# The per-layer embedding's gate as seven half-size products, with its norm weights applied at evacuations and two schedules re-paced

## The chip, the cores and the metric

One kernel runs on 1 core of a Trainium2 chip. The metric is the device time of the program in microseconds (us), the median of several runs. One more execution is profiled; all rows below are of that one.

## The reference

A decoder block on x of 512 tokens by 1024 channels, float32. Three stages follow each other: a mixer (input projection, causal pooling and a recurrent branch, merged, times `w_o`), a gated ConvFFN (`w_up`, conv, gelu, `w_down`), and a gated per-layer input embedding. What the change touches is the last stage and its join to the second:

```
x   = x + rms_norm(hid @ w_down, g_ffn_post)
ple_gate = sigmoid(rms_norm(x, g_ple_gate) @ w_ple_gate)      # 512 x 1024 @ 1024 x 1024
ple      = rms_norm(p @ w_ple_proj, g_ple_post)               # 512 x 256 @ 256 x 1024
x   = x + ple_gate * ple
```

with `rms_norm(x, g) = x * rsqrt(mean(x*x) + eps) * g`.

## The kernel before

**Numbers.** Every float32 operand of a product is split into a high part (`hi`, rounded to fp32r by a copy on ACT) and a low part (`lo = raw - hi`, a subtraction on DVE). `mm3` (lines 196 to 200) makes each product of three matmuls: hi*hi, hi*lo, lo*hi. So each 128x1024 piece of a weight costs one load, one cast on ACT and one subtraction on DVE.

**Seven products.** `wo`, `up` and `wd` are computed by a 2x2 scheme of halves (tokens, inner channels and output channels are each cut in two) with seven products in place of eight, in the order `SERIAL = (1, 2, 5, 6, 3, 7, 4)`. Products 5, 6, 7 and 4 use sums of weight blocks. `sum_in_dram` makes these sums in DRAM with DMAs on the POOL queue, the second of each pair accumulating: those of `wo` and `up` in one go once the first rsqrt is done, those of `wd` six DMAs at a time (`SUMS_EACH`), each batch released by a step of the up loop. The left operands' forms (for instance h21-h22) are made on DVE, then split. `product` walks through one product; its two banks are the first and the second 128 tokens of a half.

**Gate stage.** It isn't one of these: for each half h of the output columns and each token tile t of 128, eight inner blocks k times three matmuls of 512 columns, then sigmoid on ACT from PSUM with the row's rstd as scale, a multiply by the embedding, an add of x and a DMA out:

```python
for h in range(2):
    for t in range(NT):
        V.scalar_tensor_tensor(v, v, rp[t], gp[:, h, :], ALU.mult, ALU.mult)
        ...
                    mm3(ps[:, a:b], x3k, pick(w, (k % 2) * S + a, (k % 2) * S + b), k == 0, k == KD - 1)
                act(o[:, a:b], ps[:, a:b], AF.Sigmoid, scale=r3[t])
```

**Join.** `x3_norm(t)` forms x after the ConvFFN for tile t (two PSUM multiplies, two squares with sums on ACT, a power on POOL, two scaled adds), multiplies it by `g_ple_gate` on DVE, and takes its rstd. `x3_tile(t)` transposes the tile on the TensorE (eight 128x128 transposes, line 858) and splits what lands in PSUM. `down_product(4, ...)` is the last product of `wd`: its first bank (tile 2) ends 18 matmuls before its second (tile 3). The TensorE's order is that of the program (a manual schedule); tiles 2 and 3 are transposed inside the gate stage, after (h, t, k) = (0, 1, 2) and after (0, 1).

**Order of the other engines.** DVE, ACT, SP and POOL are scheduled by priority at build time (`tc.high_priority`, `urgent()`), then run in that order. Weights pass through six buffers each of `raw`, `hi` and `lo`; `weight(key, ahead)` prepares the next pieces. A load waits on SP until a `raw` buffer is free, and what stands behind it in SP's queue waits too.

Of the kernel before, what the change touches and what calls it, by code (L numbers as in the profile page):

```python
# [49 lines left out]
SUMS_FROM, SUMS_EACH = 2, 6  # L50
# [31 lines left out]
def block_kernel(  # L82
# [104 lines left out]

    def sub(o, a, b):
        V.tensor_tensor(o, a, b, ALU.subtract)  # L189
# [32 lines left out]
    def rows2(w, kp, h):  # L222
# [7 lines left out]
        name: w.rearrange("(q a s p) c -> q s p a c", a=2, s=2, p=P) for name, w in (("wo", w_o), ("wd", w_down))  # L230
# [22 lines left out]
    def sums_of(name):  # L253
# [7 lines left out]
        for f, start, more in ((5, 1, 0), (7, 0, 3), (6, 5, 3), (4, 6, 2)):  # L261
# [55 lines left out]
    for h in range(2):  # L317
        for kp in range(4):
            plan(("wpg", kp, h), rows2(w_ple_gate, kp, h))
# [62 lines left out]
    def prep(key):  # L382
# [28 lines left out]
        else:  # L411
            ACT.copy(hi, raw)  # L412
            with tc.high_priority(offset=2 * URGENT if key[0] == "wpg" and key[2] == 0 else 300 if key[0] == "in" and key[1] >= 12 else 0):
                sub(lo, raw, hi.bitcast(F32))
        ready[key] = (hi, lo)
# [75 lines left out]
    sum_in_dram(chain_of(sums_of("wo"), sums_of("up")), None)  # L491
# [246 lines left out]
    def ple_tile(t):  # L738
# [8 lines left out]
        outs = [slot(), slot()]  # L747
        V.tensor_copy(outs[0], pair[0])
        ACT.copy(outs[1], pair[1])
# [37 lines left out]
    of, od = {}, {}  # L787

    def o_form(f):

        h11, h12, h21, h22 = (halves(mq[k], b) for b in range(2) for k in range(2))
        v = {1: h11, 2: h12, 4: h22}.get(f)
        if f in (5, 7):
            od[f] = quad("C", F32)[:, 0:2, :].rearrange("p a (b c) -> p (a b) c", b=2)
# [9 lines left out]
        elif f == 7:  # L804
            v = od[7]
            V.tensor_tensor(v, h11, h21, ALU.subtract)
        of[f] = quad("A").rearrange("p (s a) (b c) -> p s (a b) c", s=2, b=2)
        split(of[f][:, 0], of[f][:, 1], v)

# [6 lines left out]
    for m in range(KD):  # L816
# [5 lines left out]
        if m == KD - 1:  # L822
            o_form(1)
# [10 lines left out]
        if m == KD - 1:  # L834
            o_form(2)
# [127 lines left out]

    forms = {1: h2(0, 0), 2: h2(0, 1), 4: h2(1, 1)}
# [190 lines left out]
    x3t, r3 = {}, {}  # L1155
    x3n = {}

    def x3_norm(t, pair):
        res = [x3[t // 2][:, 2 * (t % 2) + h, :] for h in range(2)]
        with tc.high_priority(offset=URGENT if t > 1 else 0):  # L1160
            add_norm(pair, (gq[:, 0, :], gq[:, 1, :]), res)
            for h in range(2):
                x3n[t, h] = nq[t // 2][:, 2 * (t % 2) + h, :]
                V.tensor_tensor(x3n[t, h], res[h], gq[:, 2 + h, :], ALU.mult)
        s3 = rstd_of(res)
# [39 lines left out]
    nq[0] = quad("C", F32)  # L1205
    for _ in down_product(7, zd, False, tail=2):
        pass
# [3 lines left out]
    load_x3(1)  # L1211
    x3_norm(0, (c11[0], c12[0]))
    for q in down_product(4, zd, False, head=3, tail=DOWN_TAIL):
        if q == 2:
            x3_norm(1, (c11[1], c12[1]))
            nq[1], gp = hquad(), hquad()
            nc.sync.dma_start(
                gp[:, 0:2, :].rearrange("p h c -> p (h c)"), rows[G_PLE_POST : G_PLE_POST + 1, :].broadcast_to([P, D])
            )
            ple = [quad("A", F32), quad("A", F32)]  # L1220
            for a in range(2):
# [3 lines left out]
                )  # L1225
        if q >= NQ:
            x3_norm(q - NQ + 2, (zd[q - NQ], q5[:, q - NQ]))
        if 1 < q < NQ + 1:
            x3_tile(0 if q < NQ else 1)


    for h in range(2):
        for t in range(NT):
            i = 2 * (t % 2) + h
            o = temp()
            v = ple[t // 2][:, i, :]
            V.scalar_tensor_tensor(v, v, rp[t], gp[:, h, :], ALU.mult, ALU.mult)
            parts = ((0, S // 2), (S // 2, S)) if (h, t) == (1, NT - 1) else ((0, S),)
            for a, b in parts:
                ps = bank()  # L1240
                for k in range(KD):
                    if (h, t, k) == (0, 1, 3):
                        x3_tile(2)
                    w = weight(("wpg", k // 2, h))
                    q = (k % 4) * P
                    x3k = pick(x3t[t, k // 4], q, q + P)
                    mm3(ps[:, a:b], x3k, pick(w, (k % 2) * S + a, (k % 2) * S + b), k == 0, k == KD - 1)
                act(o[:, a:b], ps[:, a:b], AF.Sigmoid, scale=r3[t])
                V.tensor_tensor(o[:, a:b], o[:, a:b], ple[t // 2][:, i, a:b], ALU.mult)
                V.tensor_tensor(o[:, a:b], o[:, a:b], x3[t // 2][:, i, a:b], ALU.add)  # L1250
                nc.sync.dma_start(out[t * P : (t + 1) * P, h * S + a : h * S + b], o[:, a:b])
            if (h, t) == (0, 1):
# [78 lines left out]
```

## Time and profile before

| what | us |
|---|---|
| median of 3 runs | 736.77 (735.72 to 737.68) |
| the profiled execution's own time | 737.34 |
| its span, first to last instruction | 735.6 |
| busy: TensorE (PE) / DVE / ACT / POOL | 728.2 / 577.8 / 443.6 / 82.7 |

PE is the matmul unit, PEld its weight loads, DVE the vector engine, ACT the scalar (activation) engine, POOL the GpSimd, SP the queue that issues most DMAs. A matmul's listed duration overlaps the next one's, so its cost in a row of matmuls is the distance between starts. Engine order is fixed, so an engine that waits holds up all that stands behind.

### The profile page before, as it was taken

To read this page: it belongs to the slowest core of one execution; us is meant where nothing else is said; L and a number is where in the kernel's file an instruction comes from. 1 tells how busy PE (TensorE), PEld (TensorE's weight loads), DVE (VectorE), ACT (ScalarE), POOL (GpSimd) and SP (SyncE) were. 2 spreads that over 40 slices of the span, in tenths; PEclk is the share of its full clock that TensorE was granted. 3 is DMA by queue.
4 is the path that set the end of the run, shared out by engine and by line. 5 is a ranking of instruction groups with operands and counts; after the bars stand their busy time and mean duration, and the time that the engine had idled before them with its cause. 6 is when DMAs were issued, how large, how long until landed. Compare 5 with 4: busy or idle time off the path is not lost.

```text
span 735.6 us, 11212 instructions
## 1 busy us (share of the span) xinstructions
PE 728.2 (99%) x4281; PEld 641.8 (87%) x4281; DVE 577.8 (79%) x749; ACT 443.6 (60%) x670; POOL 82.7 (11%) x107
## 2 busy tenths in 40 slices
PE   9999999999999999999999999999999999999997
PEld 7887778888888888889999999999999888888886
DVE  4896735999646577776989999979799997788852
ACT  6746779844543334477856666666577756565721
POOL 0312112100000000120002323131210000001100
PEclk9999999999999999999999999999999999999999
DMA  8999786664788997895457798979798675768011
GB/s 328 382 309 268 166 238 175 154 198 131 267 297 267 325 327 286 306 333 180 144 191 267 176 321 234 315 206 273 253 246 297 206 250 193 266 201 270 18 58 57
DMA packets 64933, 172.53 MB, mean 235 GB/s; under 512 B 5808, under 2 KB 6448, under 8 KB 64560
## 3 DMA queue, kind: packets, MB, share of 16 engines
q1 hardware_dynamic: 50336, 129.78, 50.9%
q0 software_dynamic: 14400, 41.95, 24.1%
q8 instruction: 33, 0.54, 0.3%
q14 instruction: 20, 0.16, 0.1%
q10 hardware_dynamic: 144, 0.10, 0.0%
HBM read 155.03 MB, written 58.72 MB: 291 GB/s over the span
## 4 chain that ended last, share of the span: by engine, by line
PE 87%; DMA 7%; DVE 3%; issue 1%; ACT 1%; SPq 0%; POOL 0%; DVEq 0%; ACTq 0%
PE ps L198 28%; PE ps L199 28%; PE ps L200 28%; DMA raw<-in_w_up_dram 5%; DMA C<-in_x_dram 1%; DVE lo L189 1%; PE ps L858 1%; DVE raw L348 1%; PE ps L606 1%; DMA m<-in_x_t_dram 1%; PE ps L503 1%; DVE t L1000 1%; ACT C L486 0%; ACT hi L193 0%; SPq L403 0%
## 5 line engine op out<-in xcount | busy, mean ns | idle before, releaser
L189 DVE TENSOR_TENSOR lo<-raw,hi 128x1024 fp32r<-128x1024 f32 (+2 forms) x193 | 224.5, 1183 | 50.1 <-ACT hi L412 29.4
L198 PE MATMUL ps<-A,hi 128*128 128x256 f32 (+1 forms) x608 | 197.8, 325 | 1.1 <-ACT ps L985 1.1
L199 PE MATMUL ps<-A,hi 128*128 128x256 f32 (+1 forms) x608 | 197.1, 324 | 0.0
L200 PE MATMUL ps<-A,lo 128*128 128x256 f32 (+1 forms) x608 | 197.0, 324 | 0.0
L412 ACT CAST hi<-raw 128x1024 fp32r<-128x1024 f32 (+1 forms) x112 | 113.2, 1015 | 108.1 <-PE ps L199 43.2
L198 PEld LDWEIGHTS ps<-A,hi 128*128 128x128 f32 x608 | 114.3, 188 | 12.8 <-ACT ps L985 1.5
L200 PEld LDWEIGHTS ps<-A,lo 128*128 128x128 f32 x608 | 114.1, 188 | 10.1
L199 PEld LDWEIGHTS ps<-A,hi 128*128 128x128 f32 x608 | 114.1, 188 | 9.7
L198 PE MATMUL ps<-C,hi 128*128 128x256 f32 (+1 forms) x392 | 116.9, 298 | 0.0
L200 PE MATMUL ps<-C,lo 128*128 128x256 f32 (+1 forms) x392 | 116.6, 297 | 0.0
L199 PE MATMUL ps<-C,hi 128*128 128x256 f32 (+1 forms) x392 | 116.5, 297 | 0.0
L193 ACT CAST hi<-raw 128x1024 fp32r<-128x1024 f32 x78 | 80.6, 1052 | 33.2 <-PE ps L199 23.3
L198 PE MATMUL ps<-hi,A 128*128 128x512 f32 x224 | 87.4, 390 | 0.0
L200 PE MATMUL ps<-hi,A 128*128 128x512 f32 x224 | 87.2, 389 | 0.0
L199 PE MATMUL ps<-lo,A 128*128 128x512 f32 x224 | 87.1, 389 | 0.0
L198 PEld LDWEIGHTS ps<-C,hi 128*128 128x128 f32 x392 | 73.8, 188 | 2.8 <-ACT rb L441 0.2
L199 PEld LDWEIGHTS ps<-C,hi 128*128 128x128 f32 x392 | 73.8, 188 | 2.6
L200 PEld LDWEIGHTS ps<-C,lo 128*128 128x128 f32 x392 | 73.7, 188 | 2.5
L434 POOL TENSOR_TENSOR s<-s,mhalf 128x1 f32<-128x1 f32 (+1 forms) x21 | 15.8, 754 | 353.9 <-DVE s L447 334.6
L200 PEld LDWEIGHTS ps<-hi,A 128*128 128x128 f32 x224 | 42.0, 188 | 8.8
L199 PEld LDWEIGHTS ps<-lo,A 128*128 128x128 f32 x224 | 42.1, 188 | 8.6
L198 PEld LDWEIGHTS ps<-hi,A 128*128 128x128 f32 x224 | 42.0, 188 | 8.5
(191 smaller groups left out, 1026.2 us busy)
## 6 DMA issues: line engine op xcount, KB each, us to landing
raw<-in_w_up_dram SPq DMA_DIRECT2D x46, 512.0 KB, 7.4
wdsum<-in_w_down_dram POOLq DMA_DIRECT2D x36, 512.0 KB, 13.0
raw<-in_w_in_dram SPq DMA_DIRECT2D x32, 512.0 KB, 6.6
raw<-wdsum SPq DMA_DIRECT2D x24, 512.0 KB, 4.4
raw<-in_w_down_dram SPq DMA_DIRECT2D x18, 512.0 KB, 4.6
wosum<-in_w_o_dram POOLq DMA_DIRECT2D x12, 512.0 KB, 9.8
wdsum<-wdsum POOLq DMA_DIRECT2D x12, 512.0 KB, 12.0
parts<-hi SPq DMA_DIRECT2D x10, 512.0 KB, 3.9
```

The costliest lines, as they stand in the source:

```text
L189: V.tensor_tensor(o, a, b, ALU.subtract)
L193: last_copy[0] = ACT.copy(hi, src)
L198: PE.matmul(o, ah, bh, start=start, stop=False, **kw)
L199: PE.matmul(o, ah, bl, start=False, stop=False, **kw)
L200: PE.matmul(o, al, bh, start=False, stop=stop, **kw)
L348: V.tensor_tensor(o, a, b, ALU.add)
L412: ACT.copy(hi, raw)
L434: last_pow[0] = nc.gpsimd.tensor_tensor(y, v, mhalf[:, :n], ALU.pow).ins.name
L503: PE.matmul(rx[m], a[:, o : o + P], b, start=k == 0 and i == 0, stop=k == KD - 1 and i == 2)
L606: PE.matmul(ps, bd[pr, a, o], b[pr], start=i == 0, stop=i == 2)
L858: PE.transpose(ps[:, q * P : (q + 1) * P], a[:, q * P : (q + 1) * P], ident)
L1000: V.scalar_tensor_tensor(a[:, d:], pg[:, : S - d], c1(C_FW + (2 - d) * NJ + j), a[:, d:], ALU.mult, ALU.add)
```

## The change

- The gate's product becomes seven products of halves in the `SERIAL` order: `pg_product` runs 2 banks x 4 inner blocks x 3 matmuls for each. Its weight sums are 16 more DMAs on the POOL queue, put behind those of `wo` and `up`.
- The left operand is kept whole as `xq`, and its forms are made by `pg_form` (whole) or `pg_part` (one tile of 128 tokens).
- `g_ple_gate` is applied as a per-partition scale when the transposed tile leaves PSUM (eight ACT instructions of 128 columns for each tile in place of two casts and two subtractions); `g_ple_post` when the embedding's product leaves PSUM in `ple_tile` (two DVE multiplies in place of a DVE copy and an ACT copy).
- The low parts of weight products 7 and 4 are made by ACT (minus hi) and an accumulating DMA on the POOL queue (`BY_DMA`).
- Norms of tiles 0 and 1 move before `down_product(7)`, transposes of tile 0 into it; tile 1's go to an earlier place in `down_product(4)`; tiles 2 and 3 are transposed after the first bank of gate products 1 and 2.
- `spread_rstd` (eight small matmuls that spread the first rstd) moves from after k = 2 to after k = 7 of the first input tile.
- `SUMS_EACH` is 5 in place of 6.

```diff
+BY_DMA = 7, 4
+SUMS_PG = (5, 1, 0), (6, 5, 3), (7, 0, 3), (4, 6, 2)
-SUMS_FROM, SUMS_EACH = 2, 6
+SUMS_FROM, SUMS_EACH = 2, 5
...
-    for h in range(2):
-        for kp in range(4):
-            plan(("wpg", kp, h), rows2(w_ple_gate, kp, h))
+    for f in SERIAL:
+        for q in range(pieces["wpg"]):
+            plan(("wpg", f, q), piece_of("wpg", f, q))
...
+            if key[0] == "wpg" and key[1] in BY_DMA:
+                with tc.high_priority(offset=300):
+                    ACT.copy(hi, raw)
+                    ACT.activation(lo, hi.bitcast(F32), AF.Identity, scale=-1.0)
+                    nc.gpsimd.dma_start(lo.bitcast(F32), raw, accum_op=ALU.add)
+                ready[key] = (hi, lo)
+                return
...
-    sum_in_dram(chain_of(sums_of("wo"), sums_of("up")), None)
+    sum_in_dram(chain_of(sums_of("wo"), sums_of("up"), sums_of("wpg")), None)
...
-            if m == 0 and k == 2:
+            if m == 0 and k == KD - 1:
                 spread_rstd()
...
-        outs = [slot(), slot()]
-        V.tensor_copy(outs[0], pair[0])
-        ACT.copy(outs[1], pair[1])
+        outs = [gp[:, 2 + h, :] if t == 2 else slot() for h in range(2)]
+        for h in range(2):
+            V.tensor_tensor(outs[h], pair[h], gp[:, h, :], ALU.mult)
...
     def x3_norm(t, pair):
...
-            for h in range(2):
-                x3n[t, h] = nq[t // 2][:, 2 * (t % 2) + h, :]
-                V.tensor_tensor(x3n[t, h], res[h], gq[:, 2 + h, :], ALU.mult)
...
     def x3_tile(t):
-        xq = hquad(F32R)
         for h in range(2):
-            ps = transposed(x3n[t, h])
-            x3t[t, h] = xq[:, 2 * h, :], xq[:, 2 * h + 1, :]
-            with urgent():
-                split(*x3t[t, h], ps)
+            ps = transposed(x3[t // 2][:, 2 * (t % 2) + h, :])
+            for q in range(4):
+                with urgent():
+                    ACT.activation(
+                        xq[q % 2][:, 2 * h + q // 2, t * P : (t + 1) * P],
+                        ps[:, q * P : (q + 1) * P],
+                        AF.Identity,
+                        scale=gcol[:, 4 * h + q : 4 * h + q + 1],
+                    )
...
+    def pg_part(f, i):
...
+        v, w = pd[f][:, :, t], pf[f][:, :, :, t]
+        with tc.high_priority(offset=URGENT if f != 3 else 330):
+            if f == 3:
+                ins = V.tensor_tensor(v, v, h12, ALU.add)
+                behind(ins, low[0])
+            else:
+                V.tensor_tensor(v, *((h21, h22) if f == 5 else (v, h11)), ALU.subtract)
+            split(w[:, 0], w[:, 1], v)
...
+    def out_tile(t, h, v, a=0, b=S):
+        o = temp()[:, : b - a]
+        x3h, pl = (m[t // 2][:, 2 * (t % 2) + h, a:b] for m in (x3, ple))
+        with urgent():
+            act(o, v[:, a:b], AF.Sigmoid, scale=r3[t])
+        V.scalar_tensor_tensor(o, o, rp[t], pl, ALU.mult, ALU.mult)
+        V.tensor_tensor(o, o, x3h, ALU.add)
+        nc.sync.dma_start(out[t * P : (t + 1) * P, h * S + a : h * S + b], o)
+
+    def pg_product(f, banks, start, cols=(0, S)):
+        w = [weight(("wpg", f, q), ahead=3 if f == 3 and q else q if f == 6 else 1 + q) for q in range(2)]
+        for i in range(2):
+            for a, b in zip(cols, cols[1:]) if i else ((0, S),):
+                for k in range(4):
+                    mm3(...)
+                yield i, a, b
+
+    for i, _, _ in pg_product(1, gz, True):
+        ACT.copy(g11[i], gz[i])
+        if i == 0:
+            x3_tile(2)
+            pg_part(5, 0)
+    for i, _, _ in pg_product(2, g11, False):
+        if i == 0:
+            x3_tile(3)
+            pg_part(5, 1)
+            hold["wpg", 6, 0] = low[0] = last_sub[0]
+            for n in range(2):
+                pg_part(6, n)
...
+    for i, _, _ in pg_product(5, gd5, True):
+        ACT.copy(q5[:, i], gd5[i])
+        out_tile(i, 0, g11[i])
+        x3_rstd(2 + i)
+    for i, _, _ in pg_product(6, gz, False):
+        ins = V.tensor_tensor(g11[i], q5[:, i], gz[i], ALU.subtract)
+        if i == 0:
+            hold["wpg", 3, 1] = ins.ins.name
+            for n in range(2):
+                pg_part(3, n)
+    for i, _, _ in pg_product(3, g11, False):
+        if i == 0:
+            pg_form(7)
+        out_tile(i, 1, g11[i])
+    for i, _, _ in pg_product(7, gz, False):
+        V.tensor_tensor(q5[:, i], q5[:, i], gz[i], ALU.subtract)
+        if i == 0:
+            pg_form(4)
+        out_tile(2 + i, 1, q5[:, i])
...
+    for i, a, b in pg_product(4, gz, False, (0, HALF, S)):
+        out_tile(2 + i, 0, gd5[i] if a else gz[i], a, b)
```

## Rows read from the trace of the kernel before

**Rows 1.** The page: busy time of each engine, and the TensorE clock granted in each fortieth of the span, in tenths of full speed.
```profile
PE 728.2 (99%) x4281; PEld 641.8 (87%) x4281; DVE 577.8 (79%) x749; ACT 443.6 (60%) x670; POOL 82.7 (11%) x107
...
PEclk9999999999999999999999999999999999999999
```

**Rows 2.** What the TensorE waited for in the whole span: us in total, times, longest.
```profile
PE ps L198 <- ACT ps L985: 1.1, 2, 0.8
PE ps L216 <- DVE mhalf L210: 1.1, 1, 1.1
```

**Rows 3.** The TensorE in order of time through the gate stage: start, duration, line, operation. The stage's first matmul, its two groups of transposes, the first and the last of the 48 matmuls of 256 columns that end it.
```profile
684.64 0.39 PE L200 MATMUL ps<-hi,A 128*128 128x512 f32 x1
684.87 0.39 PE L198 MATMUL ps<-hi,h 128*128 128x512 f32 x1
...
692.36 1.04 PE L858 MATMUL ps<-ident,h 128*128 128x128 f32 x8
...
696.74 1.32 PE L858 MATMUL ps<-ident,h 128*128 128x128 f32 x8
...
725.14 0.28 PE L198 MATMUL ps<-hi,h 128*128 128x256 f32 x1
...
730.77 0.28 PE L200 MATMUL ps<-hi,h 128*128 128x256 f32 x1
```

**Rows 4.** ACT and DVE after the last matmul, in order of time.
```profile
731.09 0.47 ACT L164 ACTIVATE t<-ps,r 128x256 f32<-128x256 f32 x1 [2.40 <-PE ps L200]
...
731.59 0.42 DVE L1249 TENSOR_TENSOR t<-t,A 128x256 f32<-128x256 f32 x1 [1.99 <-ACT t L164]
732.05 0.42 DVE L1250 TENSOR_TENSOR t<-t,C 128x256 f32<-128x256 f32 x1
```

**Rows 5.** Busy time by stretch in the gate stage: stretch, its length, then PE, PEld, DVE, ACT and POOL busy (instructions), granted clock, DMA share, GB/s.
```profile
685.00:700.00 15.00, 14.96 (x75) 12.16 (x74) 13.41 (x24) 11.03 (x23) 2.86 (x3) 1.00 0.00 0
700.00:716.00 16.00, 16.00 (x72) 13.27 (x71) 8.74 (x13) 4.18 (x5) 0.00 (x0) 1.00 0.18 67
716.00:731.00 15.00, 15.00 (x90) 13.25 (x88) 4.21 (x7) 1.85 (x3) 0.00 (x0) 1.00 0.16 61
```

**Rows 6.** Groups of instructions of ACT and of DVE from 640 us to the end, shapes kept apart: busy us, mean ns of one, then the idle time before them.
```profile
L412 ACT CAST hi<-raw 128x1024 fp32r<-128x1024 f32 x19 | 19.9, 1051 | 12.9 <-PE ps L200 12.7 <-ACT rb L441 0.2
L164 ACT ACTIVATE t<-ps,r 128x512 f32<-128x512 f32 x7 | 4.8, 690 | 20.1 <-PE ps L200 20.1
L193 ACT CAST h<-ps 128x512 fp32r<-128x512 f32 x8 | 4.3, 588 | 0.0
...
L164 ACT ACTIVATE t<-ps,r 128x256 f32<-128x256 f32 x2 | 0.9, 474 | 4.6 <-PE ps L200 4.6
...
L189 DVE TENSOR_TENSOR lo<-raw,hi 128x1024 fp32r<-128x1024 f32 x20 | 24.2, 1220 | 4.3 <-ACT hi L412 3.9
...
L1237 DVE SCALAR_TENSOR_TENSOR A<-A,rp,h 128x512 f32<-128x512 f32 x8 | 5.6, 742 | 0.0
...
L1249 DVE TENSOR_TENSOR t<-t,A 128x512 f32<-128x512 f32 x7 | 4.8, 689 | 14.8 <-ACT t L164 14.8
...
L1164 DVE TENSOR_TENSOR h<-C,C 128x512 f32<-128x512 f32 x4 | 2.6, 684 | 0.0
```

**Rows 7.** DVE in order of time where tiles 2 and 3 are normed: tile 2's first multiply, a weight's subtraction between its two scaled adds, the second of these, tile 3's first multiply, its two scaled adds.
```profile
681.41 0.68 DVE L850 TENSOR_TENSOR t<-ps,C 128x512 f32<-128x512 f32 x1
...
685.47 1.22 DVE L189 TENSOR_TENSOR lo<-raw,hi 128x1024 fp32r<-128x1024 f32 x1
686.61 0.75 DVE L853 SCALAR_TENSOR_TENSOR C<-t,s,C 128x512 f32<-128x512 f32 x1
...
689.67 0.68 DVE L850 TENSOR_TENSOR t<-ps,C 128x512 f32<-128x512 f32 x1
...
694.66 1.41 DVE L853 SCALAR_TENSOR_TENSOR C<-t,s,C 128x512 f32<-128x512 f32 x2 [0.72 <-POOL s L434]
```

**Rows 8.** POOL's sums (line 272): issue time of one (min/median/max ns), time from issue to landing of all 80, and, from POOL in order of time, the last sum of `up` and the next work of POOL.
```profile
L272 POOL DMA_DIRECT2D wdsum<-in_w_down_dram x36: 657/1556/3534, 390.0 to 532.5; - x36
...
DMA to landing us min/median/max: 3.8/10.7/23.7
...
152.93 1.03 POOL L272 DMA_DIRECT2D up2sum<-in_w_up_dram  x1 [4.26 <-DMA up2sum<-up2sum]
305.04 0.57 POOL L434 TENSOR_TENSOR s<-s,mhalf 128x1 f32<-128x1 f32 x1 [151.08 <-DVE s L447]
```

**Rows 9.** Busy time by stretch where the new sums would run (columns as in rows 5).
```profile
180.00:210.00 30.00, 30.00 (x134) 24.84 (x133) 20.11 (x24) 16.57 (x24) 0.00 (x0) 1.00 0.80 279
210.00:240.00 30.00, 30.00 (x134) 24.86 (x133) 17.42 (x23) 11.19 (x14) 0.00 (x0) 1.00 0.80 270
```

**Rows 10.** The chain of work that ended last, in the up loop: start, us, what; and busy time by stretch at the loop's end (columns as in rows 5).
```profile
468.77 17.10 DMA raw<-in_w_up_dram
...
508.10 18.25 DMA raw<-in_w_up_dram
...
533.51 0.36 ACT ps L985
...
540.00:560.00 20.00, 20.00 (x176) 20.00 (x175) 20.00 (x22) 15.20 (x24) 0.00 (x0) 1.00 1.06 284
```

**Rows 11.** DVE in order of time: the first use of the spread rstd.
```profile
34.33 2.47 DVE L562 TENSOR_TENSOR t<-ps,rb 128x512 f32<-128x512 f32 x4
```

More of the change, by code (lines that the diff above doesn't have):

```diff
@@ L186, in block_kernel @@
     last_copy, h2_done, z_done, q5_done = [None], [None], [None], [None]
+    last_sub, last_low = [None], [None]
+    hold = {}
     def sub(o, a, b):
-        V.tensor_tensor(o, a, b, ALU.subtract)
+        last_low[0] = V.tensor_tensor(o, a, b, ALU.subtract)
+        last_sub[0] = last_low[0].ins.name
     def split(hi, lo, src):
@@ L260, in sums_of @@
             return
-        for f, start, more in ((5, 1, 0), (7, 0, 3), (6, 5, 3), (4, 6, 2)):
+        for f, start, more in SUMS_PG if name == "wpg" else SUMS:
             for q in range(pieces[name]):
@@ L805, in o_form, with o_room @@
             v = od[7]
-            V.tensor_tensor(v, h11, h21, ALU.subtract)
+            ins = V.tensor_tensor(v, h11, h21, ALU.subtract)
+            if low[0] is not None:
+                behind(ins, low[0])
         of[f] = quad("A").rearrange("p (s a) (b c) -> p s (a b) c", s=2, b=2)
         split(of[f][:, 0], of[f][:, 1], v)
+    def o_room(f):
+        return quad("C", F32)[:, 0:2, :]
     def o_lhs(f, k, i):
@@ L1153, in load_x3 @@
         )
-    x3t, r3 = {}, {}
-    x3n = {}
+    r3 = {}
+    gcol = const.tile([P, KD], F32, tag="gcol", name="gcol")
+    nc.sync.dma_start(gcol, rows[G_PLE_GATE : G_PLE_GATE + 1, :].rearrange("o (k p) -> p (o k)", p=P))
     def x3_norm(t, pair):
@@ L1204, in block_kernel @@
         pass
-    nq[0] = quad("C", F32)
-    for _ in down_product(7, zd, False, tail=2):
-        pass
+    load_x3(1)
+    x3_norm(0, (c11[0], c12[0]))
+    x3_norm(1, (c11[1], c12[1]))
+    xq = []
+    for q in down_product(7, zd, False, tail=2):
+        if q == NQ:
+            xq += [hquad(), hquad()]
+            x3_tile(0)
+            for t in range(2):
+                x3_rstd(t)
+            act(warm, warm, AF.Sigmoid)
     for i in range(2):
@@ L1225, in block_kernel @@
                 )
+        if q == NQ:
+            pg_form(1)
+            pg_form(2)
         if q >= NQ:
             x3_norm(q - NQ + 2, (zd[q - NQ], q5[:, q - NQ]))
[L1228 to L1252, printed above, removed]
-                x3_tile(3)
@@ new lines, in out_tile @@
+    def out_tile(t, h, v, a=0, b=S):
[11 more added lines that the diff above has]
+                for k in range(4):
+                    mm3(
+                        (banks[i] if a == 0 else gd5[i])[:, a:b],
+                        pg_lhs(f, k, i),
+                        pick(w[k // 2], k % 2 * S + a, k % 2 * S + b),
+                        start and k == 0,
+                        k == 3,
+                        skip_group_check=True,
+                    )
+                yield i, a, b
@@ new lines, in block_kernel @@
+    gd5 = [bank(), bank()]
+    q5 = wpool.tile([P, 2, S], F32, tag="sum", name=nm("sum"), bufs=1)
+    for i, _, _ in pg_product(5, gd5, True):
+        with urgent():
+            ACT.copy(q5[:, i], gd5[i])
+        out_tile(i, 0, g11[i])
+        x3_rstd(2 + i)
+    for i, _, _ in pg_product(6, gz, False):
+        with urgent():
+            ins = V.tensor_tensor(g11[i], q5[:, i], gz[i], ALU.subtract)
[4 more added lines that the diff above has]
+                pg_part(3, n)
```

73 lines of the change are left out of this document (51 added, 22 removed).

## Prediction, made before the changed kernel ran

> **What bounds the kernel now.** I read the page first: the TensorE is busy 99% of the span, at the full granted clock (2.4 GHz) in every fortieth [rows 1]. A busy share can hide waits, so the next view is what the TensorE waited for: the two longest entries are 1.1 us each in the whole span, one in the up loop, one at the start [rows 2]. So from about 30 us on the end is set by the number of matmuls times their pitch, and an edit can gain only by issuing fewer of them or lose by making them wait. The third view is the TensorE in order of time through the gate stage [rows 3]. It starts at 684.87; 33 matmuls later, at 692.36, stand the first transposes, so the pitch of 512 columns is 7.49 / 33 = 0.227 us. Of 256 columns it is (730.77 - 725.14) / 47 = 0.120 us. Eight transposes move the stream by 0.8 to 1.1 us. After the last matmul come a sigmoid, a multiply, an add and a DMA [rows 4].
>
> The fourth view is how full the other engines are there: DVE 13.41 of 15 us at first, then 8.74 of 16 and 4.21 of 15; ACT 11.03, 4.18, 1.85; the DMAs at most 0.18 [rows 5]. There is room to put work in, at the back rather than at the front.
>
> **The change part by part.**
>
> *Fewer matmuls.* Before: 8 (h, t) x 8 k x 3 = 192 products of 512 columns, one eighth of them as 48 of 256: 168 x 0.227 + 48 x 0.120 = 43.9 us. After: 7 x 2 x 4 x 3 = 168, of which the last 12 as 24 of 256: 156 x 0.227 + 24 x 0.120 = 38.3 us. Gain 5.6 us [rows 3]. The transposes stay 32 in all, 16 of them in the stage. The end behind the last matmul keeps its half-width sigmoid, multiply and add: nothing.
>
> *More DVE and ACT work in a shorter stage.* DVE in the stage after, at the durations of [rows 6]: weight subtractions of products 5, 6 and 3, 6 x 1.22 = 7.3; forms 5, 6 and 3 in parts of one tile, 6 x 2 x 0.68 = 8.2; forms 7 (two full-size instructions) and 4 (one), 3 x 1.22 = 3.7; combining banks, 4 x 0.68 = 2.7; outputs, 8 x (0.74 + 0.69) = 11.4; the norms of tiles 2 and 3, about 4.3. Sum 37.6 us against 38.3 + 1.9 of transposes = 40.2 us, where before it was 26.4 [rows 5]. Starts lie a little closer than durations (the 1.22 us subtraction of [rows 7] is followed after 1.14), so DVE is some 87 to 94% full. It fits, but it no longer idles, and what matters is the handovers. With gate start B = 684.9:
>
> - Tile 2 is transposed 12 matmuls after B, at 687.6, where before it was 33 after (692.4). Its norm began at 681.41 and ended at 686.61 + 0.75 = 687.4, with a weight's subtraction of 1.14 in between [rows 7]. The two multiplies by the norm weight that followed are gone. Margin 0.2 us as measured, 1.3 without the interposed instruction.
> - Tile 3 is transposed 12 + 24 matmuls and 0.8 us later, at 693.8. Before, its norm took 689.67 to 696.0, and began 4.6 us after its bank was done because DVE was busy with tile 2 [rows 7]; two multiplies and two splits of 0.68 (2.4 us at their pitch) of that are gone or on ACT. So it ends at 691 to 693.6: margin 0.2 to 2.8.
> - Its leaving PSUM is new: eight ACT instructions of 128 columns with a pointer scale. Not in the trace; from below a quarter of the 588 ns cast of 512 columns (0.15), from above the 474 ns of 256 columns [rows 6]. The line through 690 and 474 gives 0.37 at 128 columns; with overlap I take 0.30, 2.4 us for the tile. Then subtract, cast, subtract (0.68 + 0.59 + 0.68): 694.6 + 2.4 + 2.0 = 699.0, for product 5's second bank at 700.1 (24 matmuls after the transposes). Margin 1.1, from 2.3 down to -0.3 by the bounds.
> - Product 6 at 702.8 needs a weight (1.22) and a part (2.0) that DVE starts after this: 702.2 to 702.6. Margin 0.2 to 0.6.
>
> Late next, if one of these slips, is the TensorE itself, since its order is fixed: all of the stall goes to the end. Four margins, each about or under one DVE instruction: I take 1.0 us lost, bounds 0 and 4 x 1.2 = 4.8.
>
> *Low parts by DMA.* Products 7 and 4 cost DVE nothing (4 x 1.22 = 4.9 us saved), ACT two instructions of 1.05 for each piece [rows 6], and POOL four accumulating DMAs. With six buffers, 4's second piece starts when product 6 ends; two pieces are 4.2 us of ACT; it is needed 10.9 (products 3 and 7) + 1.4 us later. That leaves 8.1 us for issue and landing. POOL's DMAs landed in 3.8 to 23.7 us, median 10.7, beside busy DMA engines [rows 8]; here these are at 0.18 or less [rows 5]. I take the low end, so nothing; at the median it is 2.6 us late, for 7 and for 4. The pieces queued behind on POOL are powers for the tiles' rstd, wanted only at the outputs.
>
> *Sixteen sums more, early.* POOL is free from 154 to 305 us; 16 sums, two at a time (a piece of each half) at the median landing of 10.7, take some 86 us and end near 240 [rows 8]. The DMA engines are 0.80 busy there [rows 9], the TensorE waits for nothing and weights are four pieces ahead: nothing, bound below. In the gate stage SP issues 14 weight loads for 8; at a share of 0.18 they are hidden.
>
> *Down sums five at a time.* The two long chains of the up loop are weight loads of 17.1 and 18.3 us behind batches of six, and they end in the loop's wait of 0.8 us [rows 2, 10]. Smaller batches can give back up to 1.1 us; but ten batches in place of eight put two where DVE is 20.00 of 20 and the DMA engines at 1.06 [rows 10], which can cost as much. I take nothing, bounds -1.1 and +1.1.
>
> *Other moves.* The spread rstd comes 15 matmuls (3.4 us) later, ready at 35.5 by the order of events; it was first used at 34.33 [rows 11], so DVE may idle 1.2 us, in a stretch where the TensorE has no wait: nothing; without that cover, 1.2. `ple_tile` gains two DVE multiplies for one DVE copy, 0.7 us for a tile, hidden by matmuls. Norms of tiles 0 and 1 are moved to earlier places and shed four multiplies (2.7 us) [rows 6]: nothing, as products 7 and 4 of `wd` (16 us each) lie over them.
>
> *Sum.* -5.6 + 1.0 = -4.6. Against the profiled execution 737.3 - 4.6 = 732.7; that execution lies 0.6 above the median, so from 736.8: **732.2 us**.
>
> **Rivals.**
>
> 1. *Half is lost in the handovers* (0.18). For it: the margins above are 0.2 to 1.5. Against it: DVE's subtractions can be put ahead of time. Three slips of 1.2 us: -5.6 + 3.6 = -2.0, 734.8; range 733.7 to 736.8.
> 2. *DVE becomes the bound: slower* (0.12). It fills 37.6 of 40.2 us, and each part alternates DVE, ACT, DVE. From the point where each of products 5, 6, 3 and 7 starts over 1.4 us late the gain is gone; at 2 us each, +8.0 - 5.6 = +2.4, 739.2. Against it: outputs (11.4 us) can wait, but for the last one.
> 3. *The sums crowd out weight loads* (0.06). Loads of 17 to 18 us cost up to 0.8 us of wait where they met six sums [rows 2, 10]; if each of the eight new pairs did the same at 180 to 240 us, 6.4 - 5.6 = +0.8, 737.6. Against it: the stretch is 0.80 busy, not 1.1.
> 4. *The low parts by DMA come late* (0.04). 2 x 2.6 us: no change of the time, 736.4. Against it: idle DMA engines.
>    A rule that would bring this about is in the Trainium skill (SBUF — State Buffer, Who interferes with whom): VectorE and GpSimd share one pair of SBUF ports as a lock, and a GpSimd-issued DMA waits for its descriptors while VectorE holds it. The page excepts two-input `tensor_tensor` by inference, and it is these that fill DVE here. The trace has POOL issues of up to 3.5 us [rows 8], but with no sign of the cause. By the page's example (2.5 us more for a DMA) the second DMA would be 5 us later, still inside the 8.1 us less 3.8 but for 0.7: the sum would be about 733.6.
> 5. *All margins hold and the up loop's wait goes as well* (0.08): -5.6 - 1.1 = -6.7, 730.1.
>
> **How the numbers follow.** The forecast has 0.52, with 730.6 to 733.7 as its own range (0 to 2.5 us lost, and a little of the up loop's wait back). Within 0.3% (2.2 us, about what a measurement of this kernel can tell) is 734.6 to 739.0. Faster: 0.52 + 0.08 + a third of rival 1 (0.06) + a sixth of rivals 3 and 4 (0.02) = 0.68. Same: the rest of 1 (0.12), half of 2 (0.06), most of the rest of 3 and 4 (0.05) = 0.23. That leaves slower 0.09. For eight in ten I leave out rival 2 and a part of 3, and the far end of 5: 730.0 to 736.6.
>
> **What would show it.** The TensorE should have 156 + 24 gate matmuls at 0.227 and 0.120 and reach its last one near 725 + 1. Right: waits in front of the transposes and of the second bank of product 5 and the first of product 6 sum to about 1 us. Rival 1 or 2: TensorE waits for DVE subtractions or ACT casts at the starts of products 5, 6, 3; rival 2 would also have DVE without idle time from 690 to the end. Rival 3: waits for loads before 305 us. Rival 4: waits for accumulating DMAs in products 7 and 4. The prediction is wrong if the stream before 684.9 gets longer, or the gate stage takes more than 43 us.

## The result, and the profile after

The changed kernel took 740.84 us in the median (738.27 to 744.26, 16 runs) against 737.43 us for the kernel before: a ratio of 1.0047, 95% interval 1.0034 to 1.006. It is slower by 3.4 us, where 4.6 us less than before were forecast. The profiled execution took 739.64 us, with a span of 737.8 (before: 735.6).

What the TensorE waited for in the changed kernel, in us in total, times, longest; it answers to [rows 2]:

```profile
PE ps L209 <- DMA lo<-raw: 3.4, 3, 1.6
PE ps L208 <- ACT A L203: 3.4, 1, 3.4
PE ps L226 <- DVE mhalf L220: 1.1, 1, 1.1
```

The wait of the up loop (the first line of [rows 2]) is gone, the one at the start stays, and two new ones of 3.4 us stand in front. Where they are, from the TensorE in order of time (start, duration, line, operation, in brackets the idle time before and what ended it):

```profile
282.66 0.58 PE L208 MATMUL ps<-hi,A 128*128 128x512 f32 x1 [3.40 <-ACT A L203]
...
283.92 0.80 PE L210 MATMUL ps<-hi,A 128*128 128x512 f32 x1 [0.25 <-DVE A L198]
...
284.94 0.63 PE L209 MATMUL ps<-lo,A 128*128 128x512 f32 x1
285.37 0.63 PE L210 MATMUL ps<-hi,A 128*128 128x512 f32 x1
...
691.31 0.93 PE L885 MATMUL ps<-ident,C 128*128 128x128 f32 x7
...
697.64 1.03 PE L885 MATMUL ps<-ident,C 128*128 128x128 f32 x8
...
719.65 0.50 PE L209 MATMUL ps<-lo,A 128*128 128x512 f32 x1 [1.59 <-DMA lo<-raw]
722.13 0.51 PE L209 MATMUL ps<-lo,A 128*128 128x512 f32 x1 [0.83 <-DMA lo<-raw]
728.89 0.50 PE L209 MATMUL ps<-lo,A 128*128 128x512 f32 x1 [1.02 <-DMA lo<-raw]
...
732.90 0.28 PE L210 MATMUL ps<-hi,A 128*128 128x256 f32 x1
```

The first is at the first product of `wo`, 400 us ahead of the gate. Matmuls of 512 columns start up to 0.43 us apart behind it (284.94, 285.37), until 286.5, instead of 0.227, so the place costs 3.4 + 0.3 + about 1.8 = some 5.5 us. The starts of the same matmuls say the same: the TensorE's order is nearly that of the kernel before up to 660 us, so matmuls can be paired, and the last one of the mixer starts 0.49 us later than before (278.87 for 278.38), one in `wo` 6.12 us later (296.06 for 289.94). By this measure the place costs 5.6 us, and the end of the up loop, where the wait went, gains 1.7. The other three are in the gate's products 7 and 4. The transposes of tiles 2 and 3 (691.31 and 697.64) wait for nothing.

The ledger of the two profiled executions: the gate stage starts 12 matmuls ahead of the transposes of tile 2, at 691.31 - 12 x 0.227 = 688.6, where it was 684.87 [rows 3]: 3.7 us lost ahead of it (5.6 at 282 us, less 1.7 in the up loop; the rest is smaller). It takes 732.90 - 688.6 = 44.3 us, where it took 45.9, and where the working had 40.2: 1.6 gained, 4.1 short. All of that stands at the three waits for `lo<-raw`: the view counts 3.4 us of idle time, and by the distance between starts they cost 1.8, 1.0 and 1.2 us, with 0.1 more behind each. The end behind the last matmul is as before. +3.7 - 1.6 = +2.1, for the spans' +2.2.

Busy time by stretch (stretch, length, then PE, PEld, DVE, ACT and POOL busy, granted clock, DMA share, GB/s); the first two lines answer to [rows 9], the last two to [rows 5]; the third is of the kernel before, the fourth of the changed one:

```profile
180.00:210.00 30.00, 30.00 (x134) 24.82 (x134) 14.96 (x21) 12.81 (x18) 6.72 (x9) 1.00 1.01 313
210.00:240.00 30.00, 30.00 (x134) 24.86 (x133) 15.11 (x19) 10.83 (x16) 1.48 (x2) 1.00 0.92 285
280.00:300.00 20.00, 20.00 (x90) 16.57 (x89) 15.45 (x15) 9.87 (x13) 0.00 (x0) 1.00 0.78 284
280.00:300.00 20.00, 17.09 (x68) 13.53 (x69) 18.99 (x20) 10.11 (x13) 0.00 (x0) 0.91 1.04 402
700.00:716.00 16.00, 16.00 (x72) 13.10 (x71) 13.86 (x18) 15.03 (x25) 0.94 (x2) 1.00 0.24 74
716.00:731.00 15.00, 11.56 (x53) 8.73 (x52) 10.26 (x19) 8.71 (x17) 4.10 (x5) 1.00 0.97 234
```

The DMA share from 180 to 240 us is 1.01 and 0.92 where it was 0.80; from 160 to 180 us, where the sums begin, it is 1.07 for 0.50. In the same 60 us DVE did 14.96 + 15.11 = 30.1 us of work where it did 37.5: 7.5 us of it were put off. They stay put off up to 280 us (from 240 to 280 DVE does 24.8 us, where it did 24.6), and from 280 to 300 it does 18.99 us, where it did 15.45.

What was put off is seen in the chain of waits between 200 and 300 us (start, us, what):

```profile
273.01 3.88 DMA parts<-lo
277.25 1.22 DVE lo L198
...
280.20 0.61 DVE m L859
...
281.44 1.22 DVE lo L198
282.66 1.21 DVE A L198
```

The last merge of the mixer that the form opening `wo` needs (`A<-m,m`), and ACT's cast of that form; the first two lines are of the kernel before, the other two of the changed one:

```profile
271.38 0.69 DVE L833 TENSOR_TENSOR A<-m,m 128x512 f32<-128x512 f32 x1
272.10 1.05 ACT L193 CAST A<-A 128x1024 fp32r<-128x1024 f32 x1 [0.63 <-DVE A L833]
...
280.83 0.69 DVE L860 TENSOR_TENSOR A<-m,m 128x512 f32<-128x512 f32 x1
281.56 1.04 ACT L203 CAST A<-A 128x1024 fp32r<-128x1024 f32 x1 [3.23 <-DVE A L860]
```

It is seen too in the writes of the early split parts to DRAM, issued by SP (issue time, least, median, most; first and last issue; time to landing of these and the parts' reads):

```profile
L347 SPq DMA_DIRECT2D parts<-hi x10: 319/332/894, 189.6 to 271.0; - x10
...
DMA to landing us min/median/max: 3.4/5.2/11.1
```

In the kernel before:

```profile
L336 SPq DMA_DIRECT2D parts<-hi x10: 319/326/360, 189.2 to 258.5; - x10
...
DMA to landing us min/median/max: 3.1/4.0/6.6
```

Weight pieces that are split early, beside the mixer's products, go to DRAM from a few shared buffers. The last write was issued at 258.5; here it is at 271.0. The subtractions (`lo L198`) of these pieces stand in DVE's order among the merges of the mixer, in both kernels alike. As they come late, the merges behind them come late: the last one that the form needs starts at 280.83, where it started at 271.38, and the TensorE, which wanted the form's cast at 279, gets it at 282.6. The 9.5 us by which the merge is late use up the 5 us that the cast was early before.

The low parts by DMA in the gate stage (line 427, POOL): issue time (least, median, most), first and last issue, and time to landing:

```profile
L427 POOL DMA_DIRECT2D lo<-raw x4: 854/867/920, 714.1 to 720.0; - x4
...
DMA to landing us min/median/max: 5.5/7.1/8.8
```

ACT, which makes minus hi ahead of each of these DMAs, casts product 7's first piece at 707.28 and comes to its minus hi 5 us later, with casts of the forms (`A<-h`) in between:

```profile
707.28 1.05 ACT L425 CAST hi<-raw 128x1024 fp32r<-128x1024 f32 x1
...
712.72 1.05 ACT L426 ACTIVATE lo<-hi 128x1024 fp32r<-128x1024 f32 x1
```

### The profile page after: what moved, and what is told of

It reads as the page before. It is cut to its first block, busy times and chain, and to the rows that moved or that the text cites. A ratio compares the mean times of both kernels' runs of the same rounds, so it can differ in the third digit from the quotient of the medians.

```text
span 737.8 us, 11253 instructions
## 1 busy us (share of the span) xinstructions
PE 724.7 (98%) x4245; PEld 637.4 (86%) x4245; DVE 582.7 (79%) x752; ACT 463.9 (63%) x716; POOL 103.9 (14%) x127
## 3 DMA queue, kind: packets, MB, share of 16 engines
q1 hardware_dynamic: 51840, 132.41, 50.7%
## 4 chain that ended last, share of the span: by engine, by line
PE 88%; DVE 4%; DMA 4%; ACT 2%; issue 1%; SPq 0%; POOL 0%; DVEq 0%; ACTq 0%
PE ps L208 29%; PE ps L210 28%; PE ps L209 28%; DVE lo L198 1%; DMA C<-in_x_dram 1%; DMA lo<-raw 1%; DVE A L198 1%; PE ps L626 1%; ACT h L1206 1%; DMA m<-in_x_t_dram 1%; PE ps L523 1%; PE ps L885 1%; DMA parts<-lo 1%; ACT hi L430 0%; DVE t L1309 0%
## 5 line engine op out<-in xcount | busy, mean ns | idle before, releaser
L198 DVE TENSOR_TENSOR lo<-raw,hi 128x1024 fp32r<-128x1024 f32 (+2 forms) x195 | 227.2, 1185 | 93.0 <-ACT hi L430 65.5
L430 ACT CAST hi<-raw 128x1024 fp32r<-128x1024 f32 (+1 forms) x114 | 115.1, 1016 | 110.6 <-issue 35.8
L208 PE MATMUL ps<-hi,A 128*128 128x512 f32 (+1 forms) x284 | 110.8, 390 | 3.4 <-ACT A L203 3.4
L209 PE MATMUL ps<-lo,A 128*128 128x512 f32 (+1 forms) x284 | 110.6, 389 | 3.4 <-DMA lo<-raw 3.4
L210 PE MATMUL ps<-hi,A 128*128 128x512 f32 (+1 forms) x284 | 110.3, 388 | 0.3 <-DVE A L198 0.3
L209 PEld LDWEIGHTS ps<-lo,A 128*128 128x128 f32 x284 | 53.6, 189 | 15.3 <-DMA lo<-raw 4.7
L208 PEld LDWEIGHTS ps<-hi,A 128*128 128x128 f32 x284 | 53.6, 189 | 14.7 <-ACT A L203 4.1
L210 PEld LDWEIGHTS ps<-hi,A 128*128 128x128 f32 x284 | 53.7, 189 | 11.6 <-DVE A L198 1.0
L454 POOL TENSOR_TENSOR s<-s,mhalf 128x1 f32<-128x1 f32 (+1 forms) x21 | 20.2, 961 | 260.9 <-DVE s L467 237.7
```

The source lines that it names most:

```text
L198: last_low[0] = V.tensor_tensor(o, a, b, ALU.subtract)
L208: PE.matmul(o, ah, bh, start=start, stop=False, **kw)
L209: PE.matmul(o, ah, bl, start=False, stop=False, **kw)
L210: PE.matmul(o, al, bh, start=False, stop=stop, **kw)
L454: last_pow[0] = nc.gpsimd.tensor_tensor(y, v, mhalf[:, :n], ALU.pow).ins.name
```

## The experiments

The kernels ran in three groups, each on one chip beside the kernel before (medians there 737.39, 736.80 and 737.21 us): before_sums, low_dve, sums_late and both_undone; sums_split, split_dve, split_low4 and split_low7; the other four. All results, with the place of the sixteen sums of the gate's weights, the products whose low parts come by DMA, and the size of a batch of down sums:

| kernel | sums | by DMA | batch | us | ratio to before, 95% |
|---|---|---|---|---|---|
| changed kernel | 16 early | 7, 4 | 5 | 740.84 | 1.0034 to 1.006 |
| before_sums | 16 early, unused | (as before) | 6 | 742.70 | 1.0058 to 1.0089 |
| low_dve | 16 early | none | 5 | 741.06 | 1.003 to 1.0063 |
| low4_early | 16 early | 4 | 5 | 738.03 | 0.9998 to 1.0018 |
| sums_late | 16 in the up loop | 7, 4 | 5 | 739.29 | 1.001 to 1.0034 |
| both_undone | 16 in the up loop | none | 5 | 738.61 | 1.0004 to 1.0026 |
| sums_split | 8 early, 8 later | 7, 4 | 5 | 733.56 | 0.9939 to 0.9963 |
| split_dve | 8 early, 8 later | none | 5 | 732.99 | 0.9935 to 0.9959 |
| split_low7 | 8 early, 8 later | 7 | 5 | 732.23 | 0.9919 to 0.9946 |
| split_low4 | 8 early, 8 later | 4 | 5 | 731.16 | 0.991 to 0.9936 |
| low4_again | the same kernel again | 4 | 5 | 731.08 | 0.991 to 0.995 |
| low4_six | 8 early, 8 later | 4 | 6 | 734.35 | 0.9942 to 0.9966 |
| low4_spread | 8 early, 8 later | 4 | 5 | 730.68 | 0.9898 to 0.9927 |

**The sums alone.** The kernel before, with nothing of the change but the sixteen sums, which nobody reads:

```diff
-        name: w.rearrange("(q a s p) c -> q s p a c", a=2, s=2, p=P) for name, w in (("wo", w_o), ("wd", w_down))
+        name: w.rearrange("(q a s p) c -> q s p a c", a=2, s=2, p=P) for name, w in (("wo", w_o), ("wd", w_down), ("wpg", w_ple_gate))
...
-    sum_in_dram(chain_of(sums_of("wo"), sums_of("up")), None)
+    sum_in_dram(chain_of(sums_of("wo"), sums_of("up"), sums_of("wpg")), None)
```

> The kernel before with one part of the change alone: the sixteen sums of the gate's weights are made on the POOL queue behind those of up, and nothing reads them. Theory (the sums crowd the writes and loads of the parts split early, so that the first product of wo is late): a TensorE wait of about 3.4 us near 280 us with a lower clock behind it, and 4 to 6 us over the kernel before. Rival (that wait comes from another edit, such as the later spread of the rstd): no wait near 280 us, and the time of the kernel before within 1 us.

742.70 us, 5.3 over the kernel before. Its TensorE waits (total, times, longest):

```profile
PE ps L198 <- ACT A L193: 2.8, 1, 2.8
...
PE ps L198 <- ACT ps L985: 0.8, 1, 0.8
PE ps L858 <- DVE h L1164: 0.7, 1, 0.7
```

Its `parts` DMAs land as late as in the changed kernel (least, median, most):

```profile
DMA to landing us min/median/max: 3.3/5.4/11.6
```

The wait is the same one, at 281.5 us, in a kernel with no other edit: the loss at 282 us is the sums' and nothing else's. The up loop's wait of 0.8 is still there, and one of 0.7 is new at tile 3's transposes in the gate stage.

A second way in which sixteen more DMAs could do this is through the build: it orders the engines, and might have ordered them anew. It did not. Up to 680 us DVE, ACT, SP and the TensorE have the same instructions in the same order in both traces, and POOL has sixteen more; only the times differ.

The size of the loss varies. By the starts of the same matmuls, as above, it is 5.0 us in this execution, 5.6 in the changed kernel's, 6.9 in low4_early's and 9.0 in low_dve's, all with the sixteen sums early.

**The sums moved into the up loop.** The changed kernel, the sixteen released at about 367 us:

```diff
-    sum_in_dram(chain_of(sums_of("wo"), sums_of("up"), sums_of("wpg")), None)
+    sum_in_dram(chain_of(sums_of("wo"), sums_of("up")), None)
...
+            if (f, p) == (5, 1):
+                sum_in_dram(sums_of("wpg"), None, q5_done[0])
```

> The changed kernel with the same sixteen sums released only by product 5 of the first regular step of the up loop (near 370 us). Theory: the wait near 280 us and the slow matmuls behind it go, 4 to 6 us less than the changed kernel, 735 to 737; where the DMA engines are full later in the up loop, up to 1.5 us of that is given back. Rival (another edit makes that wait): the time of the changed kernel, 740 to 741.

739.29 us. Its longest waits of the TensorE:

```profile
PE ps L208 <- ACT ps L1021: 3.8, 1, 3.8
PE ps L209 <- DMA lo<-raw: 3.3, 3, 1.5
```

A piece of its chain of waits (start, us, what):

```profile
378.32 8.42 DMA raw<-in_w_up_dram
```

And the stretch behind them (columns as above):

```profile
380.00:400.00 20.00, 16.19 (x116) 15.99 (x115) 13.12 (x15) 9.54 (x16) 4.57 (x6) 0.83 1.00 265
```

The wait near 280 has gone and another of 3.8 us stands at 388, where the up loop's own loads meet the row of sums at a DMA share of 1.00 (0.38 there in the changed kernel). By the starts of the same matmuls that place costs 6.7 us. The row was moved, not its cost; the 735 to 737 us that I expected did not come.

**Half early, half later.** Eight sums (those of products 5 and 6) stay early, eight go out behind the last power ahead of the up loop, some 340 to 370 us:

```diff
+    gate_sums = sums_of("wpg")
-    sum_in_dram(chain_of(sums_of("wo"), sums_of("up"), sums_of("wpg")), None)
+    sum_in_dram(chain_of(sums_of("wo"), sums_of("up"), islice(gate_sums, 8)), None)
...
+    sum_in_dram(gate_sums, None, last_pow[0])
     for kind, n in O_AFTER:
```

> The changed kernel with eight of the gate's sixteen sums where it has them and eight behind the last power of the embedding's norm (near 345 us), since sixteen in a row moved the wait to 386 us when they were released near 367 us. Theory (it is the crowding of the DMA engines by a row of sums, wherever it falls): no wait near 280 us nor near 386 us, the waits for the accumulating DMAs stay (3.3 us), 4 to 5 us less than the changed kernel: 736 to 737. Rival (the early sums do harm at half the number too): a wait of 1.5 to 3 us near 280 us, 738 to 740.

733.56 us, 0.9951. Nothing waits near 280 or 388. In its stretches from 160 to 220 us (columns as above):

```profile
160.00:180.00 20.00, 20.00 (x90) 16.57 (x89) 19.77 (x36) 6.60 (x9) 3.85 (x5) 1.00 1.09 322
180.00:200.00 20.00, 20.00 (x90) 16.57 (x89) 14.47 (x21) 11.85 (x17) 1.39 (x2) 1.00 0.97 287
200.00:220.00 20.00, 20.00 (x90) 16.56 (x89) 11.08 (x12) 8.61 (x12) 0.00 (x0) 1.00 0.86 308
```

the DMA engines are as full at first but stand at 0.86 from 200 to 220 us, where the changed kernel stands at 1.02, and the last `parts<-hi` goes out at 259.5. Against the changed kernel the ratio to before falls by 0.96%, 7 us: more than I expected (4 to 5), and within the 5.0 to 9.0 us by which the early row delays one execution or another.

**The low parts on DVE.** The changed kernel with every low part subtracted on DVE:

```diff
-BY_DMA = 7, 4
+BY_DMA = ()
```

> The changed kernel with the low parts of weight products 7 and 4 made by DVE like the others, no accumulating DMA. Theory (the three waits in products 7 and 4 are the landing of these DMAs, and DVE has room there): 3 to 4.3 us less than the changed kernel, 736.5 to 738. Rival (DVE is the bound there, 9.97 of 10 us busy from 710 us): waits of the same size for DVE's subtractions, 740 to 742.

741.06 us: no gain. None of the three waits for `lo<-raw` is left. The last matmul:

```profile
732.09 0.28 PE L210 MATMUL ps<-hi,A 128*128 128x256 f32 x1
```

And DVE in order of time to its end:

```profile
732.45 1.41 DVE L1309 SCALAR_TENSOR_TENSOR t<-t,rp,h 128x512 f32<-128x512 f32 x2
733.78 1.28 DVE L1310 TENSOR_TENSOR t<-t,C 128x512 f32<-128x512 f32 x2
734.98 0.87 DVE L1309 SCALAR_TENSOR_TENSOR t<-t,rp,h 128x256 f32<-128x256 f32 x2
735.77 0.75 DVE L1310 TENSOR_TENSOR t<-t,C 128x256 f32<-128x256 f32 x2
```

DVE runs without a gap through two whole outputs and the two halves of a third after the last matmul, and the span ends 7.8 us behind that matmul, not 4.9. The profiled execution also has a longer wait at 282 us (5.4), which is the sums' and not this edit's. From the gate's first matmul to the end of the span the low parts can be compared without that: 41.0 + 7.8 = 48.8 us here, 44.3 + 4.9 = 49.2 in the changed kernel, and 45.9 + 4.8 = 50.7 in the kernel before. So the four DMAs do save DVE time that counts; given back, it costs about what their lateness does.

**Both.** The sums in the up loop and no low part by DMA:

> Both of the above in one. Theory (the two losses add up): 731.5 to 733.5, the gain of the fewer matmuls as counted. Rival (one of the two waits is taken over by something late behind it): 735 or more.

738.61 us, with the wait of 3.9 us at 388 and the late DVE end: the two losses stand side by side, and the 731.5 to 733.5 us that I expected did not come. And with the sums split, where that wait is gone:

> The same with the low parts of weight products 7 and 4 by DVE. Theory (DVE is the bound of the gate stage then: its last add ends some 4 us after the last matmul, not 1.7): no waits of the TensorE in the stage, but 3 us between the last matmul and the end in their place: 735.5 to 737. Rival (the low parts by DMA cost nothing in the end): the time of the same kernel with accumulating DMAs, or more.

732.99 us, against 733.56 with both by DMA: again the same within a tenth of a per cent.

**One product each.** If DMA for both is too much for the DMAs and DVE for both too much for DVE, one of each should beat them (edits against sums_split):

```diff
-BY_DMA = 7, 4
+BY_DMA = (4,)
```

> The same with the low parts of product 4 alone by accumulating DMA, those of 7 by DVE. Theory (DVE has room for 2.4 of the 4.9 us, ACT has 2.1 us less, so that 4's DMAs are issued earlier and land in time): no wait over 0.5 us in products 7 and 4, the last add about 2 us after the last matmul: 731.5 to 734. Rival (an accumulating DMA is late wherever it is): waits of 1 us for each of 4's pieces, 735 or more.

```diff
-BY_DMA = 7, 4
+BY_DMA = (7,)
```

> The same with the low parts of product 7 alone by accumulating DMA, those of 4 by DVE. Theory: 7's two waits stay (about 2.4 us with the uneven matmuls behind them), and DVE ends 1 to 2 us late: 735 to 737, over the kernel that has product 4 alone by DMA. Rival (which of the two products it is makes no difference): the same time as that kernel.

731.16 us for 4 and 732.23 for 7. The DMAs of split_low4:

```profile
L427 POOL DMA_DIRECT2D lo<-raw x2: 874/898/922, 712.5 to 714.1; - x2
...
DMA to landing us min/median/max: 4.6/5.3/6.0
```

They land in time, with no wait for `lo<-raw`, and from the gate's first matmul to the end it takes 46.9 us where sums_split takes 49.3 and split_dve 48.8. Its interval, 0.991 to 0.9936, is clear of that of sums_split and touches that of split_dve. Its profiled execution, the slowest of its six, also waits 1.4 us for a bank at 379.3, in the up loop; low4_again, the same kernel, does not.

With 7 alone one wait of 2.06 us stays at 713.85: product 7 comes first and its DMAs are issued as late as the forms ahead of them on ACT allow (707.8 and 708.7; they land in 6.0 to 7.6 us). The matmuls behind it start 0.42 us apart, and the stage takes 49.1 us to the end, no less than with both by DMA. Its 0.9919 to 0.9946 is not clear of any of the other three. The late end on DVE that I expected for it isn't there: 5.0 us behind the last matmul.

**Three parts apart.** On one more chip, split_low4 again as the base, then (edits against it) with the sums back early, with six down sums to a batch, and with the spread of the scale back at its old place:

> The kernel of split_low4 once more, as the base of the next three: eight sums of the gate's weights early and eight behind the last power before the up loop, low parts by DMA in product 4 alone. All theories: as before, ratio 0.991 to 0.994 to the kernel before, some 5 to 6 us under it.

```diff
-    gate_sums = sums_of("wpg")
-    sum_in_dram(chain_of(sums_of("wo"), sums_of("up"), islice(gate_sums, 8)), None)
+    sum_in_dram(chain_of(sums_of("wo"), sums_of("up"), sums_of("wpg")), None)
...
-    sum_in_dram(gate_sums, None, last_pow[0])
```

> The changed kernel with all sixteen sums early, as it had them, and low parts by DMA in product 4 alone. If the early row of sixteen sums costs what the profiles show near 280 us, whatever the low parts do, this stands some 5 to 7 us over low4_again: 736.5 to 738.5, with a TensorE wait of 2.8 to 5 us near 280. If the two losses only came together (rival), it keeps most of the gain: 732 to 733.5.

```diff
-SUMS_FROM, SUMS_EACH = 2, 5
+SUMS_FROM, SUMS_EACH = 2, 6
```

> low4_again with the down sums six at a time, as the kernel before had them. If five at a time took the up loop's wait away, this is 0.8 to 1.1 us over low4_again, with a wait for ACT or a weight near the loop's end. If the number does nothing (as I predicted), within 0.5 us of it.

```diff
-            if m == 0 and k == KD - 1:
+            if m == 0 and k == 2:
```

> low4_again with the spread of the norm's scale back behind the third group of matmuls of the first block, as the kernel before had it. As I predicted (hidden): within 0.5 us of low4_again, DVE's first use of the spread scale about 1 us sooner or the same. Rival: the place sets DVE's work at the start, and with it a wait of the TensorE: 1 us or more apart.

731.08, 738.03, 734.35 and 730.68 us. The row of sums early costs 7 us by the medians and 5.8 by the ratios here too, so the two losses add up whatever the low parts do; the wait of low4_early is 3.92 us at 282.6. Six to a batch costs 3.3 us by the medians and 1.8 by the ratios, where the prediction took nothing and I expected at most 1.1. The times alone don't settle it: the two intervals overlap, and two of the six executions of low4_again (734.05 and 735.23) are as slow as those of low4_six. The traces say more: the three with six to a batch all wait at the end of the up loop, 0.8 to 2.1 us, and of the eleven with five none does. In low4_six the TensorE waits, and the matmuls of 256 columns behind that start 0.21 us apart, not 0.11:

```profile
532.48 0.39 PE L208 MATMUL ps<-A,hi 128*128 128x256 f32 x1 [2.13 <-ACT ps L1017]
...
533.29 0.41 PE L209 MATMUL ps<-A,hi 128*128 128x256 f32 x1
533.51 0.42 PE L210 MATMUL ps<-A,lo 128*128 128x256 f32 x1
```

The loads of `up` from 430 to 545 us landed in 6.2, 9.8 and 19.7 us there (least, median, most), and with five to a batch (low4_again) in

```profile
DMA to landing us min/median/max: 4.1/7.8/12.7
```

The kernel before, with six, has 5.7, 9.6 and 18.2 us, and the changed kernel, with five, 4.4, 7.6 and 12.7.

The spread's place does nothing that can be told. Its scaled products on DVE (line 583) start at 37.42 us in low4_again and at 34.01 in low4_spread, the TensorE doesn't wait for them in either, and the times are 0.4 us apart.

## Why the prediction was wrong

**Fewer matmuls, -5.6: right.** The pitches are the same (13 of them from 688.13 to 691.07, 0.226 us each). low4_again, in which little else is lost, is 6.1 us under the kernel before by the medians and 5.2 by the ratio. The count gives 5.9: 5.6, and 1.7 at the end of the up loop, less 1.4 of waits in its own gate stage (0.43 and 1.01 us).

**Handovers, +1.0: not in the changed kernel.** None of the four margins that I worked out ran out: no wait stands at either group of transposes, at product 5's second bank or at product 6 (tile 3's eight scaled copies out of PSUM took 2.17 us, where I took 2.4). The changed kernel loses nothing there. split_low4 and low4_again lose 1.4 us, at the starts of product 3 and of product 4's second bank, to banks that DVE has not yet written or ACT not yet copied; that this is near my 1.0 is luck. Rival 1 didn't happen.

**Sixteen sums, "nothing": the step that failed first.** I counted when the sums would end (near 240; the last was issued at 210.7) and asked whether a weight load of the running products would be late. Loads did land later (6.6 us in the median from 160 to 280 us, and 12.4 at most, where it was 4.9 and 7.8), but the TensorE waited for none. I left out who else uses the DMA engines there: the pieces split early, whose loads and writes to DRAM go through the same stretch and whose DVE work stands ahead of the merge that the form opening `wo` needs; that form is due at 279 us. A share of 0.80 that becomes 1.0 didn't stop the TensorE at once; it put off 7.5 us of DVE work, which fell due 40 to 80 us later on an engine that works in order. Rival 3 had the cause, but looked for the wait at 180 to 240 us, priced it by a load's lateness (0.8 us a pair) and not by what queues behind it, and had a chance of 0.06; that its 6.4 us come near the measured loss is luck. Measured: 5.3 us alone (before_sums), 6 to 7 in the changed kernel (by sums_split, and by low4_early against low4_again). What the sums and the other transfers contend for, the engines' time or the memory's, no run here separates.

**Low parts by DMA, "nothing": the second.** I took the least landing of [rows 8], 3.8 us, because the DMA share of the gate stage was 0.18 [rows 5]. That share was of a stage without these DMAs. With all four it is 0.97 from 716 to 731, and in low_dve, without them, it is 0.14:

```profile
716.00:731.00 15.00, 14.98 (x73) 12.32 (x72) 14.13 (x22) 6.96 (x13) 1.84 (x2) 1.00 0.14 53
```

So four DMAs fill (0.97 - 0.14) x 15 / 4 = 3.1 us of all sixteen engines each, an estimate. Issued within 6 us, they queue on one another and land in 5.5 to 8.8 us. Their issue is late too: ACT is busy 15.03 of 16 us from 700 to 716, so the first goes out at 714.07 for a matmul that wanted it at 718.06. Product 7, the earlier of the two, was never worked out for itself; I gave only 4's time. At the median landing my own figure was 2 x 2.6 = 5.2 us. Measured: three waits of 3.4 us, which cost 4.1 by the starts, and 2.4 us between both by DMA and 4 alone. Rival 4 had 0.04.

The rule quoted beside rival 4 (the Trainium skill, SBUF — State Buffer, Who interferes with whom) has a DMA issued by GpSimd stall while VectorE holds the shared ports. The runs show no sign of it: the issues took 0.85 to 0.92 us with DVE busy 13.86 of 16 us and 10.26 of 15, less than the early sums' median of 1.06 us, and two DMAs in place of four landed sooner (4.6 to 6.0 us) though DVE had more to do; that agrees with the page's exception for `tensor_tensor`.

**Down sums five at a time, 0 with bounds -1.1 and +1.1: mis-sized.** At the end of the up loop the changed kernel gains 1.7 us by the starts, and in the shorter kernel low4_six loses 2 to 3 us against five.

**Other moves, nothing: right for the spread** (0.4 us apart). It came later than I said, 37.4 for 35.5, and was hidden all the same. The moved norms and the products in `ple_tile` were not undone by themselves; no wait of the TensorE stands at them.

**DVE as the bound (rival 2)** does not happen while the DMAs take the low parts, and does in low_dve and split_dve, where the end comes 7.8 us after the last matmul, 3 us late. The mechanism was real, and the four DMAs bought it off at a like price.

Together, in the profiled executions: -5.6 (matmuls) + 5.6 (sums) + 4.1 (low parts) - 1.7 (up loop) = +2.4, for the +2.2 of the spans. The medians are 3.4 us apart; the profiled execution lies 1.2 us under its median, and the loss at 282 us varies by more than that. Both signs of being wrong that the prediction named came: the stream is longer ahead of the gate (688.6 for 684.9), and the gate takes 44.3 us, over 43. What stays open is why the early row costs 5 us in one execution and 9 in another; and how the landing of a low part divides between queueing on the engines and POOL's own work, which was not measured (with two DMAs 0.9 us apart, split_low7, they still took 6.0 to 7.6 us).

A version that beats both kernels came out of it: eight sums early and eight behind the last power, low parts by DMA for product 4 alone, batches of five: 731.1 us on two chips, 0.991 to 0.995 of the kernel before. With the spread at its old place it read 730.7.

## What to carry to other kernels

Work put on DMA engines that have room is not free because the bound engine waits for nothing there: list everything that uses the transfers in that stretch, and follow each user to its next due time, however far off. A DMA share read from a stage without the new transfers isn't the share they will meet; add their own time first. Where two engines can each take a piece of work and either alone runs late, divide the pieces, by which is due last.

## What the runs showed of the hardware

- An accumulating DMA of 512 KB from SBUF to SBUF landed in 4.6 to 6.1 us with two issued 1.6 us apart (split_low4, low4_again), in 6.0 to 7.6 with two 0.9 us apart (split_low7), and in 5.4 to 8.8 us with four in 6 us (the changed kernel, sums_split).
- Behind the waits of 3.40 us at 282 us and 2.13 us at 532 us the TensorE came back at its lower level, 1.2 GHz: matmuls of 512 columns 0.43 us apart and of 256 columns 0.21, where they are 0.227 and 0.11 to 0.12 at 2.4. In the changed kernel that added about 1.8 us to the 3.4. Behind the wait of 2.06 us in split_low7 it did too (0.42 us apart, granted clock 0.81 from 711 to 720 us). In the stretch of the waits of 1.59, 0.83 and 1.02 us (716 to 731) the granted clock stayed at 1.00.
